# Full-height low-rank products for the decay, and a planner that keeps a waiting unit's step behind the main chain's

## The chip, the cores and the metric

The kernel runs on one core of one Trainium2 chip. The metric is the device time of one execution in microseconds (us); the time of a version is the median of several runs.

## The reference

One block of a hybrid network on a sequence of 1024 tokens with 1024 channels: a normalised and modulated input is projected by `w_in`, a forget-gated attention (8 heads) and an RWKV-7 recurrence (8 heads of 64) work on parts of the projection, their outputs are gated, merged and projected, and a gated convolutional feed-forward part follows. The lines that the change touches:

```python
r, k, v, xw, xa, xg = _split(p, RWKV_SPLITS)           # xw, xa: 64 columns each
w_log = -jax.nn.softplus(-(w0 + jnp.tanh(xw) @ w2)) - 0.5
decay = jnp.exp(-jnp.exp(w_log))
a = jax.nn.sigmoid(a0 + xa @ a2)
g = jax.nn.sigmoid(xg) @ g2
...
def step(state, inp):                                  # over 1024 tokens, 8 heads
    sa = jnp.einsum('bhvk,bhk->bhv', state, a_t)
    state = state * w_t + sa[..., None] * b_t + v_t[..., None] * k_t
    y_t = jnp.einsum('bhvk,bhk->bhv', state, r_t)
```

`w2` and `a2` are 64 x 512, so `tanh(xw) @ w2` and `xa @ a2` are low-rank products with 64 terms in each sum.

## The kernel before

All matrix products of weight are done with operands that are split into a high and a low fp32r half. A product is then hi x hi + hi x lo + lo x hi, three matmuls of 128x512 per 128 terms of the sum.

**Low-rank products.** `w2` is loaded twice into one tile, so that rows 0 to 63 and rows 64 to 127 hold the same 64 weight rows (the first 512 columns belong to the decay, the other 512 to `a`). `w2h` is its high half. `xs2[j]` holds the high half of the activation on 64 rows and its low half on the other 64. One matmul of `w2h` with `xs2[j]` over 128 rows therefore gives hi x hi + hi x lo at once. The third part, lo x hi, uses `w2l` (128x512: the low half of each weight on the 64 rows where `xs2[j]` has its high half) and takes only these 64 rows of both. `lora` runs this for 4 groups of 128 output columns and 2 halves of the sequence; each of the 8 steps issues 4 matmuls (`zp` in the trace) and 2 activations `z` on ScalarE, and then steps aside for 1000 ns of planned time.

**The planner.** The order of TensorE's instructions is written out by the class `Weave`. It keeps a planned clock `now` and a list of chains (Python generators). A chain issues instructions and yields how long its results will take. `run` always takes, among the chains that are due, the one with the lowest priority number; where no chain is due, `fill` issues matmuls of the queue (filler: projections that nothing waits for soon) until the next chain is due. The queue holds the `qk`, `v` and 16 gate projections (48 matmuls each, 24 for either half of the sequence). What of it the recurrence doesn't use is left to the attention; the gates appear as `gt` in the first and as `rk_ps` in the second.

**The recurrence.** Its 8 units (4 head pairs x 2 halves) go through two chains. `pre_chain` (number 2) makes a unit's operands: sums for the norm (`ssq`), masks of the products of `ar` and `bk` (`p`, written to `E`), a solve of 31 steps on VectorE (lines L779 and L781) that goes through DRAM before (`sm`, `M32`) and after (`se`, `TT`), transposes (`vt`, `at`, `tb`), `q`, and a sum `bs`. `main_chain` (number 1) then takes the unit: a transpose `X` of `TT` on VectorE (L836), `xi`, `zi`, `uw`, `mz`, and 8 steps of the state `S` (`sp`, `yp`; the state is scaled on VectorE at L901), then norms `mu` and `va`. While the main chain has no unit it asks again every 200 ns.

Between recurrence and attention, `weave.finish()` issues the rest of the gate that has been begun. The attention of the last head ends the stage, and the merge (`br`) begins.

VectorE, ScalarE, GpSimd and the DMA queue of SyncE are ordered by the tile scheduler in the first two stages, which follows the order in which TensorE's instructions were issued; in the attention VectorE and ScalarE keep the written order.

Of the kernel before, what the change touches and what calls it, by code (L numbers as in the profile page):

```python
# [10 lines left out]
F32R = mybir.dt.float32r  # L11
AF = mybir.ActivationFunctionType
ALU = mybir.AluOpType
# [3 lines left out]
S = 1024  # L17
# [30 lines left out]
class Weave:  # L48
# [27 lines left out]
    def add(self, load, run):  # L76
        self.queue.append((load, run))
# [35 lines left out]

        self.live.append([self.now + wait, 0, chain])

    def run(self, chains):

        self.live = [[self.now, 1 + i, g] for i, g in enumerate(chains)]
        while self.live:
            due = min((c for c in self.live if c[0] <= self.now), key=lambda c: (c[1], c[0]), default=None)  # L120
            if due is None:
                self.fill(min(c[0] for c in self.live))
                continue
            wait = next(due[2], None)
            if wait is None:
                self.live.remove(due)
            else:
                due[0] = self.now + max(wait, 0.0)
# [3 lines left out]
def hybrid_block(ctx: ExitStack, tc: tile.TileContext, a, out):  # L132
    nc = tc.nc
    weave = Weave()
# [11 lines left out]
    def f32(ap):  # L146
        return ap.bitcast(F32)
# [197 lines left out]
    with ExitStack() as es:  # L345
# [54 lines left out]
        HS = (slice(0, 64), slice(64, 128))  # L400
# [4 lines left out]
        xp = lg_st.enter_context(tc.tile_pool(name="xp", bufs=1))  # L405
        xwa = xp.tile([128, S], F32, name="xwa")
        xg = xp.tile([128, S], F32, name="xg")
        w2h = xp.tile([128, S], F32R, tag="w2h", name="w2h")
        w2l = xp.tile([128, 512], F32R, name="w2l")
        g2 = xp.tile([128, 512], F32, name="g2")  # L410


        with tc.tile_pool(name="st", bufs=1) as st, tc.tile_pool(name="stp", bufs=2, space=PS) as stp, \
# [111 lines left out]
            w2 = rp.tile([128, S], F32, tag="raw", name="w2")  # L525
# [19 lines left out]
                for kt in range(KT):  # L545
                    low_part(kt, half, (2,))
            nc.scalar.copy(w2h, w2)
            for j in range(2):
                rs, js = slice(j * 64, j * 64 + 64), slice(j * 512, j * 512 + 512)
                nc.gpsimd.tensor_tensor(w2l[rs, :], w2[rs, js], f32(w2h[rs, js]), op=ALU.subtract)  # L550
            for j, dst in enumerate((xwa, xg)):
                low_out(j, dst)
            nc.scalar.preload_act_table_set("sigmoid_and_others")
# [6 lines left out]
        with tc.tile_pool(name="lg", bufs=1, reuse_waits="tile") as lg, \  # L560
                tc.tile_pool(name="md", bufs=1, reuse_waits="tile") as md:

            xs2 = [lg.tile([128, S], F32R, tag=f"xs{j}", name=f"xs{j}", bufs=1) for j in range(2)]
            for j in range(2):
                rs, ro = slice(j * 64, j * 64 + 64), slice(64 - j * 64, 128 - j * 64)
# [20 lines left out]
            def lora(p, parts):  # L586

                zs = [lg.tile([128, S], F32, tag="z", name=f"z{i}_{p}", bufs=4) for i, _, _, _ in parts]
                for hf in range(2):
                    cs = slice(hf * NH, hf * NH + NH)  # L590
                    pss = [gen(f"zp{i}_{p}{hf}") for i, _, _, _ in parts]
                    for ps, (_, prods, _, _) in zip(pss, parts):
                        for n, (w, x) in enumerate(prods):
                            mm(ps, w[:, p * 128 : p * 128 + 128], x[:, cs], start=n == 0, stop=n == len(prods) - 1)
                    for z, ps, (_, _, _, bias) in zip(zs, pss, parts):
                        if bias is None:
                            nc.vector.tensor_copy(z[:, cs], ps)
                        else:
                            last[:] = [nc.scalar.activation(z[:, cs], ps, AF.Sigmoid, bias=V(bias, p))]
                    if len(parts) > 1 or p > 0:  # L600
                        next(mods, None)
                    yield 1000
                for z, (i, _, _, _) in zip(zs, parts):
                    nc.sync.dma_start(d_lora[i, p], z)
# [3 lines left out]
            def lora_chain():  # L608
                yield 13000
                for p in range(4):  # L610
                    yield from lora(p, [(j, [(w2h[:, j * 512 : j * 512 + 512], xs2[j]), (w2l[HS[j]], xs2[j][HS[j]])], None, b) for j, b in enumerate(("w0", "a0"))])
                use_ln_exp(last[0])
                prods = split_g()
                yield from forget()
                mod_out(2)
                next(mods, None), next(mods, None)
                for p in range(4):
                    yield from lora(p, [(2, prods, None, None)])
                mod_out(5)
                while got[0, 0] < 3:  # L620
                    weave.step()
                yield 0
# [341 lines left out]
        def pre_chain():  # L964
            for k, (p, hf) in enumerate(order):
                while got[p, hf] < 3:
                    weave.step()
                yield from pre(k, p, hf)
                if p < 3:
                    weave.first.extend(rkv_items(p + 1, hf))  # L970
                yield 0

        def main_chain():
            for k, (p, hf) in enumerate(order):
                while (p, hf) not in units:
                    yield 200
                yield from main(k, p, hf)
                yield 0

        weave.run([main_chain(), pre_chain()])  # L980
    rk_st.close()


# [473 lines left out]
    due = []  # L1457
# [514 lines left out]
```

## Time and profile before

| | |
|---|---|
| time, median of 3 runs | 1701.49 us (1699.32 to 1701.51) |
| profiled execution, its own time | 1699.35 us |
| span of the profiled execution | 1697.6 us |
| TensorE busy in the span | 1649.3 us (97%) |
| VectorE / ScalarE / GpSimd busy | 72% / 48% / 8% |
| mean granted clock of TensorE | 0.991 |

The page says that TensorE is busy nearly all the time, and the chain of work that ended last is 82% TensorE. A matmul's record overlaps the next one's, so durations of single matmuls are longer than the time that each adds; the distance from one start to the next is what counts. The stages, by the timeline: up to 75 us load and norm, 75 to 149 the low-rank products among projections, 149 to 645 the recurrence, 645 to 861 the attention, and then the merge and the feed-forward part.

### The profile page before, as it was taken

The page shows a single profiled execution, that of the slowest core. Times are in us where ns is not written, and L with a number is a line of the kernel's source. Part 1 is how long each engine was busy: PE and PEld are TensorE (multiplying, and loading weights), DVE is VectorE, ACT ScalarE, POOL GpSimd, SP SyncE. Part 2 cuts the span into 40 slices and gives each one's busy share as a digit, 9 for nine tenths or more (in the row PEclk, how much of TensorE's full clock was granted, in tenths as well). Part 3 has the DMA queues.
Part 4 walks back from the last instruction along what each step waited for, and adds up shares of the span by engine and source line. Part 5 has one row for each costly group of instructions (what it writes and reads, how often), then busy time and mean ns, then how long its engine had stood idle before and what let it go on. Part 6 is the DMA issues. An engine that isn't in the chain of part 4 may idle for free.

```text
span 1697.6 us, 26285 instructions
## 1 busy us (share of the span) xinstructions
PE 1649.3 (97%) x9886; PEld 1351.7 (80%) x9886; DVE 1218.1 (72%) x2402; ACT 810.7 (48%) x1482; POOL 127.8 (8%) x151
## 2 busy tenths in 40 slices
PE   7999999999999998999989999999999999999998
PEld 7767877787877777888878888888888888888886
DVE  4776787778776624888767534897777777787677
ACT  5553334334354555766732223654444444454455
POOL 0010101111111001212022000000000000000000
PEclk9999999999999999999999999999999999999999
DMA  8487743533332226543177611133332233484463
GB/s 329 145 310 207 194 129 93 137 104 113 99 114 79 93 70 163 145 125 109 39 291 267 223 62 63 50 106 103 121 106 100 93 118 106 158 290 149 128 215 109
DMA packets 120975, 239.87 MB, mean 141 GB/s; under 512 B 39888, under 2 KB 48336, under 8 KB 120848
## 3 DMA queue, kind: packets, MB, share of 16 engines
q1 hardware_dynamic: 112896, 220.94, 39.5%
q0 software_dynamic: 7952, 17.25, 3.8%
q8 instruction: 78, 1.28, 0.3%
q14 instruction: 49, 0.40, 0.1%
HBM read 172.59 MB, written 65.54 MB: 140 GB/s over the span
## 4 chain that ended last, share of the span: by engine, by line
PE 82%; DVE 9%; DMA 4%; ACT 3%; issue 1%; SPq 1%; DVEq 0%; ACTq 0%
PE X L140 13%; PE D L140 12%; PE Y L140 6%; PE gt L140 6%; PE wo L140 5%; PE br L140 5%; PE ps_rkv L140 5%; PE qk L140 4%; PE W L140 3%; PE rk_ps L140 3%; PE v L140 2%; PE ov L140 2%; PE lg L140 2%; PE sp L140 2%; PE tr L140 2%; PE tp L144 2%
## 5 line engine op out<-in xcount | busy, mean ns | idle before, releaser
L140 PE MATMUL D<-op,op 128*128 128x512 f32 x924 | 209.8, 389 | 0.0
L140 PEld LDWEIGHTS D<-op,op 128*128 128x128 f32 x924 | 173.4, 188 | 36.3 <-DVE op L1235 0.3
L140 PE MATMUL X<-T_m,S 128*128 128x512 f32 x440 | 107.2, 390 | 0.2
L140 PEld LDWEIGHTS X<-T_m,S 128*128 128x128 f32 x440 | 82.5, 188 | 18.2 <-ACT x L1511 0.6
L1234 ACT CAST op<-g 128x512 fp32r<-128x512 f32 x77 | 47.8, 621 | 73.4 <-PE D L140 48.3
L1235 DVE TENSOR_TENSOR op<-g,op 128x512 fp32r<-128x512 f32 x77 | 53.0, 688 | 41.3 <-ACT op L1234 41.2
L1471 DVE SCALAR_TENSOR_TENSOR c<-ab,vec,c 128x512 f32<-128x512 f32 x88 | 65.9, 750 | 19.5 <-ACT c L1474 17.9
L779 DVE TENSOR_TENSOR t<-E,M 128x60 f32<-128x60 f32 (+24 forms) x248 | 57.2, 231 | 31.5 <-DMA M<-sm 26.2
L273 DVE TENSOR_TENSOR lo_in<-raw_in,hi_in 128x512 fp32r<-128x512 f32 x84 | 56.4, 706 | 30.0 <-PE gt L140 12.1
L1435 DVE TENSOR_TENSOR S<-ur,S 128x512 fp32r<-128x512 f32 x66 | 45.5, 691 | 35.4 <-ACT S L1431 35.2
L1431 ACT CAST S<-ur 128x512 fp32r<-128x512 f32 x66 | 41.0, 622 | 55.6 <-DVE ur L1424 30.6
L1435 DVE TENSOR_TENSOR A<-ur,A 128x512 fp32r<-128x512 f32 x64 | 44.0, 688 | 31.2 <-ACT A L1431 31.0
L271 ACT CAST hi_in<-raw_in 128x1024 fp32r<-128x1024 f32 x42 | 43.9, 1048 | 46.9 <-PE ps_rkv L140 16.9
L140 PE MATMUL Y<-T_h,A 128*128 128x512 f32 x264 | 63.4, 389 | 0.0
L140 PE MATMUL Y<-T_h,S 128*128 128x512 f32 x264 | 63.3, 389 | 0.0
L1051 ACT ACTIVATE P<-lg,nm 128x896 f32<-128x896 f32 (+3 forms) x64 | 47.5, 743 | 28.6 <-DVE nm L1047 19.6
L140 PE MATMUL X<-B_b,A 128*128 128x512 f32 x252 | 60.8, 390 | 0.0
L140 PE MATMUL W<-B_f,A 128*128 128x512 f32 x252 | 60.6, 389 | 0.0
L781 DVE TENSOR_TENSOR E<-E,t 128x60 f32<-128x60 f32 (+24 forms) x248 | 53.7, 216 | 5.8
L140 PEld LDWEIGHTS Y<-T_h,A 128*128 128x128 f32 x264 | 49.6, 188 | 10.3
L140 PEld LDWEIGHTS Y<-T_h,S 128*128 128x128 f32 x264 | 49.6, 188 | 10.3
L1431 ACT CAST A<-ur 128x512 fp32r<-128x512 f32 x64 | 39.9, 623 | 34.5 <-PE X L140 31.5
(469 smaller groups left out, 4163.9 us busy)
## 6 DMA issues: line engine op xcount, KB each, us to landing
raw_in<-in_w_in SPq DMA_DIRECT2D x50, 512.0 KB, 4.1
wm<-in_w_mod SPq DMA_DIRECT2D x48, 512.0 KB, 6.7
ur<-in_w_up SPq DMA_DIRECT2D x44, 512.0 KB, 4.1
g<-d_g SPq DMA_DIRECT2D x35, 512.0 KB, 3.7
d_g<-gs SPq DMA_DIRECT2D x44, 256.0 KB, 2.0
d_g<-c SPq DMA_DIRECT2D x33, 256.0 KB, 4.5
d_st<-qh SPq DMA_DIRECT2D x64, 128.0 KB, 2.5
d_gate<-gs SPq DMA_DIRECT2D x32, 256.0 KB, 3.0
```

Of the source, the lines that this page charges most:

```text
L140: nc.tensor.matmul(o, lhsT, rhs, start=start, stop=stop, skip_group_check=more)
L144: nc.tensor.transpose(o, i, eye)
L271: nc.scalar.copy(hi, raw)
L273: nc.vector.tensor_tensor(lo[:, c : c + NH], raw[:, c : c + NH], f32(hi[:, c : c + NH]), op=ALU.subtract)
L779: tt(tv, E32[:, 0:J, s : s + 1].to_broadcast([128, J, W]), M32[:, s : s + 1, s + 1 : 32].to_broadcast([128, J, W]), op=ALU.mult)
L781: tt(E32[:, 0:J, s + 1 : 32], E32[:, 0:J, s + 1 : 32], tv, op=ALU.add)
L1051: nc.scalar.activation(e[:, 0:n], lg[:, 0:n], AF.Exp, bias=nm[:, 0:1], accum_out=nm[:, 1:2])
L1234: nc.scalar.copy(hi, src)
L1235: tt(lo, src, f32(hi), op=ALU.subtract)
L1431: nc.scalar.copy(hi, src)
L1435: tt(lo, src, f32(hi), op=ALU.subtract)
L1471: stt(c, ab[:, x + hf * NH : x + hf * NH + NH], V("conv_w", 22 * x + i), c, op0=ALU.mult, op1=ALU.add)
```

## The change

Two edits. The first makes `w2l` a full 128x1024 tile (the low half of both copies of all weights) in another pool, written by one instruction on GpSimd, and takes all 128 rows of it and of `xs2[j]`: hi x lo's missing partner, lo x lo, is added to the sum by it. The second gives `run` an argument `near`: a chain of number 2 that is due is held, with filler instead, as long as a chain of number 1 comes due later than now and sooner than `near` (1300 ns) after the time at which the held chain came due. Only the recurrence passes it.

```diff
-    def run(self, chains):
+    def run(self, chains, near=0.0):
...
+            if near and due[1] == 2:
+                first = min((c[0] for c in self.live if c[1] == 1), default=0.0)
+                if self.now < first < due[0] + near:
+                    self.fill(first)
+                    continue
             wait = next(due[2], None)
...
-        w2l = xp.tile([128, 512], F32R, name="w2l")
...
-            for j in range(2):
-                rs, js = slice(j * 64, j * 64 + 64), slice(j * 512, j * 512 + 512)
-                nc.gpsimd.tensor_tensor(w2l[rs, :], w2[rs, js], f32(w2h[rs, js]), op=ALU.subtract)
...
+            w2l = lg.tile([128, S], F32R, tag="w2l", name="w2l", bufs=1)
+            nc.gpsimd.tensor_tensor(w2l, w2, f32(w2h), op=ALU.subtract)
...
-  [(w2h[:, j * 512 : j * 512 + 512], xs2[j]), (w2l[HS[j]], xs2[j][HS[j]])]
+  [(w2h[:, j * 512 : j * 512 + 512], xs2[j]), (w2l[:, j * 512 : j * 512 + 512], xs2[j])]
...
-        weave.run([main_chain(), pre_chain()])
+        weave.run([main_chain(), pre_chain()], 1300)
```

(The two lines with `w2h` are the lists of products in `lora_chain`, without the rest of the line.)

The order of instructions moves in the recurrence and behind it. Three places follow. The first is on TensorE where the main chain takes the seventh unit (`xi`, `zi` and `uw` with index 0) while the pre chain is at the end of the eighth (`tb`, `q` and `bs` with index 1). Before:

```order
L144 MATMUL tb_11_6040<-cst,bk_1_5674 128x64
L140 MATMUL q_1_6059<-UV_1_5842,E_1_5840 64x64 x16
L140 MATMUL va_1_6010<-Zts_1_6011,blk_r 128x512
L140 MATMUL va_1_6010<-Mts_1_6012,blk_r 128x512
L140 MATMUL xi_0_6097<-X_0_6094,E_0_5165 32x32 x16
L140 MATMUL gt_0_6037<-u_hi,hi_in_5774 128x512 x7
L140 MATMUL gt_0_6037<-u_lo,hi_in_5774 128x512 x5
L140 MATMUL zi_0_6128<-TT_0_5309,X_0_6094 32x32 x16
L140 MATMUL bs_1_6077<-cum_1_6078,blk_r 128x512
L140 MATMUL bs_1_6077<-en_1_6079,blk_r 128x512
```

The same place now, from `va` on (16 rows of `tb` stand where the three dots are):

```order
L146 MATMUL va_1_5948<-Zts_1_5949,blk_r 128x512
L146 MATMUL va_1_5948<-Mts_1_5950,blk_r 128x512
L146 MATMUL xi_0_6093<-X_0_6090,E_0_5311 32x32 x16
...
L146 MATMUL q_1_6132<-UV_1_5882,E_1_5880 64x64 x16
L146 MATMUL zi_0_6155<-TT_0_5463,X_0_6090 32x32 x16
L146 MATMUL gt_1_6068<-u_lo,hi_in_5716 128x512 x7
L146 MATMUL gt_1_6068<-u_hi,lo_in_5717 128x512 x3
L146 MATMUL uw_00_6185<-QA_0_5312,TT_0_5463 64x128 x8
L146 MATMUL uw_04_6197<-QA_0_5312,TT_0_5463 64x128 x8
L146 MATMUL bs_1_6150<-cum_1_6151,blk_r 128x512
L146 MATMUL bs_1_6150<-en_1_6152,blk_r 128x512
```

The next unit's steps have gone behind the main chain's: `tb` and `q` from ahead of `va` and `xi` to behind them, `bs` from behind `zi` to behind `uw`. Counted over the whole recurrence, TensorE goes from a projection or sum (fp32r) to a step of the chains (fp32) or back 223 times instead of 237.

The second place is on TensorE at the end of the attention, the last head (`tp` are transposes of the probabilities, `ov` their products with the values, `rk_ps` the last gate). Before:

```order
L140 MATMUL rk_ps<-u_lo,hi_in_8734 128x512 x7
L140 MATMUL ov<-th_20_9220,vh_8676 128x256
L140 MATMUL ov<-tl_20_9228,vh_8676 128x256
L140 MATMUL ov<-th_20_9220,vh_8676 128x256
L140 MATMUL ov<-tl_20_9228,vh_8676 128x256
L144 MATMUL tp_22_9240<-cst,P_4_9117 128x128
L144 MATMUL tp_22_9240<-cst,P_5_9141 128x128 x2
L140 MATMUL ov<-th_21_9225,vh_8676 128x256
L140 MATMUL ov<-tl_21_9233,vh_8676 128x256
L140 MATMUL ov<-th_21_9225,vh_8676 128x256
L140 MATMUL ov<-tl_21_9233,vh_8676 128x256
L140 MATMUL rk_ps<-u_hi,lo_in_8735 128x512 x7
```

The same place now:

```order
L150 MATMUL tp_22_9247<-cst,P_4_9161 128x128
L150 MATMUL tp_22_9247<-cst,P_5_9184 128x128 x2
L146 MATMUL ov<-th_20_9231,vh_8746 128x256
L146 MATMUL ov<-tl_20_9237,vh_8746 128x256
L146 MATMUL ov<-th_20_9231,vh_8746 128x256
L146 MATMUL ov<-tl_20_9237,vh_8746 128x256
L146 MATMUL ov<-th_21_9245,vh_8746 128x256
L146 MATMUL ov<-tl_21_9252,vh_8746 128x256
L146 MATMUL ov<-th_21_9245,vh_8746 128x256
L146 MATMUL ov<-tl_21_9252,vh_8746 128x256
```

The last gate's matmuls are gone from here. In all, 48 gate matmuls have moved from the attention (336 before, 288 now) into the recurrence and the stretch right behind it (432 before, 480 now). The attention's order on TensorE is the same as before up to the place where the last gate began, and without filler from there on.

The third place is on the DMA queue of SyncE after the input's loads (`raw_in` are columns of `w_in`, `wm` of `w_mod`). Before:

```order
L259 DMA raw_in_643<-in_w_in 128x1024
L259 DMA raw_in_650<-in_w_in 128x1024
L259 DMA raw_in_688<-in_w_in 128x1024
L217 DMA wm_0_759<-in_w_mod 128x1024
L217 DMA wm_1_775<-in_w_mod 128x1024
L217 DMA wm_2_795<-in_w_mod 128x1024
L259 DMA raw_in_726<-in_w_in 128x1024
```

Now:

```order
L265 DMA raw_in_642<-in_w_in 128x1024
L265 DMA raw_in_649<-in_w_in 128x1024
L223 DMA wm_0_758<-in_w_mod 128x1024
L223 DMA wm_1_774<-in_w_mod 128x1024
L223 DMA wm_2_794<-in_w_mod 128x1024
L265 DMA raw_in_687<-in_w_in 128x1024
L632 DMA wr<-in_w_f 128x64
L637 DMA bf<-in_b_f 8x1
L265 DMA raw_in_725<-in_w_in 128x1024
```

The third load of `w_in` has gone behind three loads of `w_mod`, and the fourth, which takes the buffer that `w2` leaves, behind two small ones.

More of the change, by code (lines that the diff above doesn't have):

```diff
@@ L610, in lora_chain @@
                 for p in range(4):
-                    yield from lora(p, [(j, [(w2h[:, j * 512 : j * 512 + 512], xs2[j]), (w2l[HS[j]], xs2[j][HS[j]])], None, b) for j, b in enumerate(("w0", "a0"))])
+                    yield from lora(p, [(j, [(w2h[:, j * 512 : j * 512 + 512], xs2[j]), (w2l[:, j * 512 : j * 512 + 512], xs2[j])], None, b) for j, b in enumerate(("w0", "a0"))])
                 use_ln_exp(last[0])
```

## The prediction

> **What bounds the kernel now.** I read the page first, then the chain of waits, then the timeline of TensorE in the three stretches that the change touches.
>
> ```profile
> span 1697.6 us, 26285 instructions
> PE 1649.3 (97%) x9886; PEld 1351.7 (80%) x9886; DVE 1218.1 (72%) x2402; ACT 810.7 (48%) x1482; POOL 127.8 (8%) x151
> PE 82%; DVE 9%; DMA 4%; ACT 3%; issue 1%; SPq 1%; DVEq 0%; ACTq 0%
> ```
>
> TensorE (PE) is busy 97% of the span and is 82% of the chain that ended last. All matmuls before are there after, so the time can change in three ways only: a matmul takes another time, TensorE waits more or less, or its clock differs. The 48 us of the span in which it isn't busy are the stock that reordering can draw on. In the recurrence (149 to 645 us) the waits of TensorE are, with line, releaser, total, times and longest:
>
> ```profile
> PE xi L140 <- DVE X L836: 3.2, 2, 1.9
> PE sp L140 <- DVE S L901: 3.2, 3, 2.2
> PE at L144 <- DVE E L759: 1.8, 1, 1.8
> PE ps_rkv L140 <- DVE k L368: 1.7, 1, 1.7
> ```
>
> That is 9.9 us in a stage of 496. Whatever the planner's new rule is worth by removing waits, it is not more than that.
>
> **The low-rank products, worked out.** The `zp` tiles, minimum, median and maximum in ns, and how the products stand in the timeline (start, length, instruction):
>
> ```profile
> L140 PE MATMUL zp<-xgs,g2s x24: 389/389/792, 132.4 to 146.0; 128*128 128x512 f32 x24
> L140 PEld LDWEIGHTS zp<-xs,w2h x16: 186/187/188, 89.6 to 110.7; 128*128 128x128 f32 x16
> L140 PE MATMUL zp<-xs,w2h x16: 387/446/502, 89.8 to 110.7; 128*128 128x512 f32 x16
> L140 PEld LDWEIGHTS zp<-xs,w2l x16: 182/182/183, 90.1 to 111.1; 64*128 64x128 f32 x16
> L140 PE MATMUL zp<-xs,w2l x16: 491/498/502, 90.1 to 111.1; 64*128 64x512 f32 x16
> ...
> 80.52 1.98 PE L140 MATMUL ps_rkv<-u_hi,hi_in 128*128 128x512 f32 x8
> 82.33 1.98 PE L140 MATMUL ps_rkv<-u_lo,hi_in 128*128 128x512 f32 x8
> ...
> 92.69 0.39 PE L140 MATMUL zp<-xs,w2h 128*128 128x512 f32 x1
> 93.01 0.49 PE L140 MATMUL zp<-xs,w2l 64*128 64x512 f32 x1
> 93.43 0.50 PE L140 MATMUL zp<-xs,w2h 128*128 128x512 f32 x1
> 93.86 0.50 PE L140 MATMUL zp<-xs,w2l 64*128 64x512 f32 x1
> 94.29 1.43 PE L140 MATMUL ps_rkv<-u_hi,lo_in 128*128 128x512 f32 x5
> 95.56 0.39 PE L140 MATMUL zp<-xs,w2h 128*128 128x512 f32 x1
> ```
>
> A run of 128-row matmuls starts one every (82.33 - 80.52) / 8 = 0.2265 us. In the low-rank step the starts are 0.32, 0.42, 0.43 and 0.43 us apart, and the projections behind it take 1.27 instead of 5 x 0.2265 = 1.13: the step with its 5 projections lasts 95.56 - 92.69 = 2.87 us where 9 evenly spaced matmuls would last 2.04. So changing between 64 and 128 rows costs 0.83 us a step. There are 8 steps (16 `w2h` matmuls, 2 a step), and TensorE waits for nothing else in them: 8 x 0.83 = **6.6 us** less. Bounds: 0, if the distance doesn't come from the 64 rows, and 6.6. I take the full value, because the `zp<-xgs` products, same code, same neighbours and 128 rows, have a median of 389 ns, not 446 or 498.
>
> By the Trainium skill ("TensorE: Matmul & The Clock Gate", sections "LDWEIGHTS (loading the stationary operand)" and "Why this matters for your kernels") a weight load depends on its columns and not on its rows, and a matmul with few rows in the sum takes the same time as one with 128; this term would then be 0. The trace agrees for the load (182 against 187 ns) and not for the matmul (0.43 against 0.2265 us from start to start).
>
> The new `w2l` instruction comes later, since its tile takes memory of the first stage, which is in use until the last low products before 75.08:
>
> ```profile
> L550 POOL TENSOR_TENSOR w2l<-w,w2h x2: 1290/1292/1294, 70.7 to 72.1; 64x512 fp32r<-64x512 f32 x2
> 75.08 1.98 PE L140 MATMUL ps_rkv<-u_hi,hi_in 128*128 128x512 f32 x8
> 73.38 0.33 SPq L259 DMA_DIRECT2D raw_in<-in_w_in  x1
> 86.72 2.12 PE L140 MATMUL ps_rkv<-u_hi,hi_in 128*128 128x512 f32 x8 [0.60 <-DVE k L368]
> ```
>
> Two pieces of 512 columns took 1.29 us each; one of 1024 columns takes 2.6 by columns, 5.2 if twice the elements cost twice. It ends by 80.3 at the latest, and its first reader is at 90.1 (table above), so its cover is 9.8 us and it costs 0. Queued behind it are the one-column copies on GpSimd and, on SyncE, the fourth load of `w_in`, which needs `w2`'s buffer. The third load, now behind three loads of `w_mod`, started at 73.38 and is read at 86.72: 13 us of cover. Both 0; without cover, each us of lateness would be one of TensorE.
>
> **The planner's rule: mode changes.** A change from a projection to a step of the chains is not free even without a wait:
>
> ```profile
> 577.43 1.66 PE L140 MATMUL gt<-u_hi,lo_in 128*128 128x512 f32 x6
> 579.02 0.34 PE L140 MATMUL sp<-UV,E 128*64 128x64 f32 x4
> ```
>
> Six `gt` need 6 x 0.2265 = 1.36 us, and the next start comes after 1.59: 0.23 us for the way there and next to nothing for the way back. The order has 223 such changes instead of 237, so 7 ways there fewer: 7 x 0.23 = **1.6 us** less.
>
> **The 48 gate matmuls that move.** Holding steps makes the recurrence use more filler. 48 matmuls, 48 x 0.2265 = **10.9 us**, come into the recurrence and the stretch behind it: TensorE is nearly always busy there, so they cost their whole time. What the attention's end gives back for them is the open term. Its order is unchanged up to 832.17, so I read what follows:
>
> ```profile
> core 0: us, PE busy (x) PEld busy (x) DVE busy (x) ACT busy (x) POOL busy (x), PEclk, DMA share, GB/s
> 645.40:832.17 186.77, 176.01 (x1077) 153.32 (x1075) 148.41 (x301) 123.44 (x281) 33.54 (x39) 0.99 0.45 124
> 832.17:856.23 24.06, 23.05 (x137) 19.42 (x136) 17.25 (x33) 14.79 (x32) 0.00 (x0) 1.00 0.12 44
> 860.64:863.90 3.26, 3.26 (x8) 2.61 (x9) 0.00 (x0) 0.46 (x1) 2.51 (x2) 0.56 0.87 236
> ...
> 855.83 0.40 PE L140 MATMUL rk_ps<-u_hi,lo_in 128*128 128x512 f32 x1
> 860.64 3.43 PE L140 MATMUL br<-fx,hi_br 128*128 128x512 f32 x8 [4.41 <-ACT hi_br L1208]
> ...
> 856.03 0.37 ACT L1118 COPY o<-ov 64x256 f32<-64x256 f32 x1 [2.06 <-PE ov L140]
> 858.59 0.60 ACT L1131 CAST fx<-o 128x512 fp32r<-128x512 f32 x1
> 859.98 1.12 ACT L1208 CAST hi_br<-raw_br 128x512 fp32r<-128x512 f32 x2
> ...
> 856.43 0.42 DVE L1120 TENSOR_TENSOR o<-o,ov 64x256 f32<-64x256 f32 x1 [1.87 <-ACT o L1118]
> ```
>
> (In rows of stages: length, busy time of each engine with its instructions, granted clock, DMA share, GB/s.) From 832.17 to the first `br` at 860.64 are 28.47 us, and 48 x 0.2265 = 10.9 of them are the gate that moves. Without it TensorE has some 12 us of work here and waits for VectorE and ScalarE instead. Floor: VectorE's own 17.25 us. A stage doesn't reach that: in the attention as a whole VectorE is busy 148.41 of 186.77 us, 79%, and 17.25 / 0.79 = 21.8. I take the middle of 17.25 and 21.8, **19.5 us** to the end of the last `ov`.
>
> Then comes the wait for `hi_br`. The last `ov` ends at 855.83; ScalarE's `o` starts 0.20 later, VectorE's `o` at 856.43 and ends at 856.85; `fx` would need 0.60 and `hi_br` 0.62 of ScalarE. Before, the last gate's activations stood ahead of both and `br` started at 860.64; without them it starts 0.20 + 0.40 + 0.42 + 0.60 + 0.62 + some 0.05 = **2.3 us** after the last `ov`. So the stretch lasts 19.5 + 2.3 = 21.8 instead of 28.47: **6.7 us** back. Ends: 17.25 + 2.3 = 19.6, 8.9 back; or no end of the stretch moves, 0 back.
>
> After the wait of 4.41 us the granted clock was 0.56, and eight `br` matmuls took 3.26 us instead of 8 x 0.2265 = 1.81. If the wait is 2.3 us, I take this restart to go: **1.45 us** less (0 if the clock falls all the same).
>
> **Other moved work.** Filler's weight loads move with it; they run ahead of their use, and at the end SyncE's queue has the last gate's store no longer ahead of the merge's loads: 0. Waits inside the recurrence are dealt anew, since VectorE's order changes with TensorE's; the 9.9 us of the first table say how much is at stake. I take no change, with 4 us either way.
>
> **The sum.** -6.6 (low-rank steps) - 1.6 (mode changes) + 10.9 (48 gate matmuls earlier) - 6.7 (the attention's end) - 1.45 (clock) = **-5.45 us**. Against the profiled execution's 1699.35 us (span 1697.6 and 1.75 around it) that is 1693.9. Its time is at the lower edge of the three runs shown (1699.32 to 1701.51, median 1701.49), and a median is asked, so I put the sum on the median: **1696.0 us**. What a measurement of this kernel can tell from no change is about 0.2%, 3.4 us.
>
> **Rivals.**
>
> *A unit's solve comes too late (slower).* The rule holds a step of the next unit by up to 1.3 us. Up to the load of `M32` that starts the solve a unit has five such steps, so its `X` can come up to 5 x 1.3 = 6.5 us later against the main chain. What there is to spare, at the third unit:
>
> ```profile
> 321.50 0.44 DVE L836 STREAM_TRANSPOSE X<-TT 32x256 f32<-32x256 f32 x1 [0.59 <-DMA TT<-se]
> 328.74 0.69 PE L140 MATMUL xi<-X,E 32*32 32x32 f32 x32
> ```
>
> `X` ends at 321.94 and `xi` starts at 328.74: 6.8 us. For: the margin is nearly the size of the delay, and TensorE, in order, waits with all that is behind `xi`. Against: it takes every step held in full. Price: what the first unit pays in the table of waits, 3.2 us a unit. Four late units: 12.8 - 5.45 = +7.35, 1708.8 us. It decides from 8.9 us on, three units. Chance 0.12.
>
> *The attention's end gives nothing back (same).* If VectorE and ScalarE behind the last head set the end as it is, the 28.47 us and the restart stay: -6.6 - 1.6 + 10.9 = +2.7, 1704.2 us. For: the end is a chain through three engines. Against: VectorE's 17.25 us leave room, and four ScalarE activations of the gate vanish from ahead of `hi_br`. Chance 0.13.
>
> *64 rows cost nothing (same).* If the distance of 0.43 us comes from something else in that stretch, such as its full DMA queues, the first term goes: -5.45 + 6.6 = +1.15, 1702.6 us. The page named above would have it so. Against: neighbours of 128 rows keep 0.2265 there. Chance 0.06.
>
> *The rule removes the waits (faster).* With the main chain's work first on VectorE, all of the 9.9 us but the first unit's 3.2 go: -5.45 - 6.7 = -12.15, 1689.3 us. For: `S` and the masks `E` wait behind a next unit's work on VectorE. Against: nothing keeps other work, such as the weights' low halves, out of VectorE's way. Chance 0.13.
>
> **How the numbers follow.** My sum has 0.52: 0.47 of it faster by over 0.2%, 0.05 within it. The waits removed, 0.13, are faster. Nothing given back, 0.13: 0.10 within, 0.03 slower. 64 rows free, 0.06: within. Late solve, 0.12: slower. What is left, 0.04, is a handful of small new waits that add up: slower. Faster 0.60, within 0.2% 0.21, slower 0.19. The range goes from the waits removed, 1688, to nothing given back, 1705; it leaves out the late solve, the small waits and the edges of the others, some 2 in 10.
>
> **What would show it.** Low-rank steps: 64x512 is gone from `zp`, starts are 0.2265 us apart, and what follows stands 6 to 7 us earlier at about 112 us. The recurrence's end then comes some 3 us later than before (-6.6 - 1.6 + 10.9, part of it behind the end). The stretch from `lg` of the last head to `br` shows waits of TensorE of some 7 us where there was one of 4.41, and the first `br` runs at full clock. I am wrong if `zp` keeps its distances, if TensorE's waits in the recurrence leave 9.9 us by more than 4, or if that last stretch lasts under 19 or over 25 us.

## The result, and the profile after

The changed kernel takes 1710.46 us (median of 6 runs, 1708.94 to 1714.42) against 1701.1 us before: ratio 1.0061, 95% interval 1.0048 to 1.0075. It is slower by some 9 us; 1696.0 and a range up to 1705 had been forecast. (The 1701.1 us are the median of six runs of the kernel before, three more than in the table ahead.)

The part on the low-rank products did what was said. Of `zp`'s 16 products with `w2l`, the starts before ran from 90.1 to 111.1 us; after (the tile's group on TensorE: min/median/max ns, first and last start):

```profile
L146 PE MATMUL zp<-xs,w2l x16: 389/389/389, 88.0 to 102.8; 128*128 128x512 f32 x16
```

No 64-row matmul is left, and the 21.0 us are 14.8. The loss is behind that. TensorE's stages before (stretch, its length, busy time and instructions of each engine, granted clock, DMA share, GB/s): the filler ahead of the first unit's `vt`, the recurrence to the last `sp`, from there to the first `rk_ps`, from that to the first `lg`, the attention to its last `lg`, from that to the first `br`:

```profile
146.40:178.80 32.40, 32.40 (x161) 25.62 (x160) 18.87 (x28) 10.97 (x18) 2.92 (x4) 1.00 0.77 221
178.80:632.90 454.10, 443.48 (x4151) 353.53 (x4151) 319.67 (x937) 197.38 (x347) 50.19 (x69) 1.00 0.38 110
632.90:647.90 15.00, 15.00 (x73) 12.37 (x74) 4.20 (x6) 9.69 (x15) 6.45 (x7) 1.00 0.46 138
647.90:661.20 13.30, 10.09 (x45) 8.02 (x44) 4.03 (x6) 5.37 (x9) 2.15 (x4) 1.00 1.17 262
661.20:841.10 179.90, 172.26 (x1070) 150.56 (x1069) 151.50 (x310) 122.13 (x282) 29.80 (x35) 0.99 0.37 106
841.10:860.60 19.50, 14.21 (x91) 12.10 (x89) 10.91 (x20) 13.39 (x28) 0.00 (x0) 0.99 0.12 41
```

The same six stages after, then the first eight `br` and the first 2.5 us behind the longest wait:

```profile
138.80:178.40 39.60, 39.60 (x192) 31.61 (x192) 19.98 (x30) 13.16 (x21) 5.03 (x9) 1.00 0.78 228
178.40:640.40 462.00, 443.85 (x4141) 355.63 (x4141) 325.69 (x939) 199.37 (x350) 49.77 (x69) 0.99 0.38 105
640.40:661.60 21.20, 21.20 (x100) 17.52 (x99) 6.17 (x9) 12.05 (x20) 8.11 (x9) 1.00 0.70 189
661.60:679.70 18.10, 11.88 (x44) 9.35 (x44) 2.58 (x4) 5.35 (x9) 0.38 (x1) 0.81 0.76 195
679.70:858.30 178.60, 168.90 (x1051) 147.47 (x1050) 150.16 (x307) 122.20 (x282) 28.80 (x34) 0.99 0.34 98
858.30:871.50 13.20, 9.90 (x62) 8.28 (x61) 9.87 (x19) 8.07 (x18) 0.00 (x0) 0.87 0.26 76
871.50:874.80 3.30, 3.30 (x9) 2.57 (x10) 0.14 (x1) 0.46 (x1) 2.51 (x2) 0.57 0.99 338
673.48:676.00 2.52, 2.52 (x6) 2.04 (x7) 1.37 (x3) 1.72 (x3) 0.00 (x0) 0.50 0.23 66
```

The ledger of the two spans (1697.6 and 1707.2 us): -7.7 up to the first `f` of the forget gate (105.1 instead of 112.8), +7.3 from there to the first `vt`, +7.9 in the recurrence, +6.2 to the first `rk_ps`, +4.8 to the first `lg`, -7.6 in the rest of the attention, -1.3 from `br` to the end: +9.6. Filler accounts for part of it. The order puts 32 more matmuls ahead of the recurrence; by the rows 27 more stand behind it (100 instead of 73), which leaves 11 fewer in it; together these are the 48 that left the attention. The recurrence thus lasts 7.9 us longer with 2.5 us (11 x 0.2265) less to do. TensorE stood for 18.15 us in it instead of 10.62 (length less busy time), and it was busy 443.85 us instead of 443.48 although it had those 2.5 us less to do. What it takes for the same matmuls is called pace below. TensorE's waits, by name (us, times, longest), of the whole execution:

```profile
PE rk_ps L146 <- ACT gm L1161: 7.4, 3, 6.2
PE sp L146 <- DVE S L905: 5.5, 5, 2.0
PE ps_rkv L146 <- DVE t L783: 5.1, 1, 5.1
PE uw L146 <- ACT TT L856: 4.0, 2, 2.8
PE br L146 <- ACT hi_br L1212: 2.1, 1, 2.1
```

Two places stand out: `ps_rkv` and `uw` in the recurrence, which waited for other things or not at all before, and `rk_ps` at the beginning of the attention.

**In the recurrence, VectorE stands before a load.** Around the second `uw` wait, in the timeline (start, duration, what ended the wait in brackets):

```profile
444.23 1.72 SPq L775 DMA_DIRECT2D M<-sm  x4
...
449.59 0.19 DVE L783 TENSOR_TENSOR t<-E,M 128x31 f32<-128x31 f32 x1 [7.14 <-DMA M<-sm]
450.04 0.69 DVE L345 SCALAR_TENSOR_TENSOR gs<-gt,gs 128x512 f32<-128x512 f32 x1
450.76 0.63 ACT L346 ACTIVATE gs<-gs 128x512 f32<-128x512 f32 x1 [3.35 <-DVE gs L345]
451.30 0.73 ACT L856 COPY TT<-zi 32x256 f32<-32x256 f32 x2
451.70 0.43 PE L146 MATMUL uw<-QA,TT 64*64 64x128 f32 x2 [2.78 <-ACT TT L856]
```

The first instruction of a next unit's solve stands next on VectorE and waits 7.14 us for `M`. Behind it stands the gate's `gs`; for that ScalarE waits, and behind ScalarE's `gs` stands the copy of `TT` that the main chain's `uw` needs. The wait of `ps_rkv` has the same source by a longer way, in the timeline 100 us earlier:

```profile
330.40 0.19 DVE L783 TENSOR_TENSOR t<-E,M 128x31 f32<-128x31 f32 x1 [5.66 <-DMA M<-sm]
333.33 0.69 DVE L938 TENSOR_TENSOR o<-y,gg 128x512 f32<-128x512 f32 x1
334.05 0.34 SPq L939 DMA_DIRECT2D d_orw<-o  x1
334.97 0.51 SPq L712 DMA_DIRECT2D cum<-d_lora  x1
339.49 1.23 DVE L715 TENSOR_TENSOR_SCAN cum<-cst,cum 128x512 f32<-128x512 f32 x1 [0.77 <-DMA cum<-d_lora]
340.74 0.63 ACT L718 ACTIVATE el<-cum 128x512 f32<-128x512 f32 x1 [2.51 <-DVE cum L715]
341.80 1.98 ACT L277 CAST hi_in<-raw_in 128x1024 fp32r<-128x1024 f32 x2
342.88 3.06 PEld L146 LDWEIGHTS ps_rkv<-u_hi,hi_in 128*128 128x128 f32 x8 [5.35 <-ACT hi_in L277]
```

VectorE stands 5.66 us before `M`, so `o` comes late; SyncE's queue holds the store of `o` and behind it the load of `cum`; ScalarE waits for `cum`, and behind its `el` and `en` stands the cast `hi_in` of the weights that the projection needs. (The table of waits names a `t` of VectorE that ended at about the same time; the weight load of the same matmul, the last row, names `hi_in`.)

VectorE's whole wait for `M` (us, times, longest), after and then before:

```profile
DVE t L783 <- DMA M<-sm: 31.3, 7, 7.1
```

```profile
DVE t L779 <- DMA M<-sm: 26.2, 7, 5.5
```

The stall is not new, but what stood behind it was needed less.

**The clock makes these waits dearer.** Three slices of the recurrence in the changed kernel:

```profile
300.00:350.00 50.00, 44.64 (x486) 39.80 (x485) 33.87 (x105) 17.22 (x35) 5.16 (x8) 0.97 0.41 111
450.00:500.00 50.00, 48.30 (x348) 38.02 (x349) 39.95 (x117) 21.41 (x33) 6.89 (x11) 0.97 0.33 101
500.00:550.00 50.00, 47.92 (x465) 36.37 (x465) 38.33 (x109) 26.24 (x46) 6.38 (x7) 0.97 0.24 69
```

In the kernel before the same three stretches of time have a granted clock of 1.00. Within them the clock falls behind three waits: in the 3.4 us behind that of 5.14 us (`ps_rkv`) it was 0.50, behind that of 2.78 us (`uw`) 0.56, and behind one of 1.97 us for `S` at 530.02, which was not traced to `M`, it was 0.59. As an estimate from the rows, 3 x 50 x 0.03 = 4.5 us of the pace are lost so.

**At the junction, the gate's stores meet two heads' loads.** The queues of GpSimd and SyncE and ScalarE's waits, in the timeline:

```profile
651.61 0.72 POOL L997 DMA_DIRECT2D stA<-d_st  x1
...
654.23 0.32 SPq L347 DMA_DIRECT2D d_gate<-gs  x1
...
659.75 8.71 SPq L347 DMA_DIRECT2D d_gate<-gs  x2
...
664.81 0.60 ACT L342 ACTIVATE gs<-gt 128x512 f32<-128x512 f32 x1 [5.08 <-DMA d_gate<-gs]
672.34 0.60 ACT L1160 ACTIVATE gs<-rk_ps 128x512 f32<-128x512 f32 x1 [4.22 <-DMA d_gate<-gs]
```

GpSimd issues head 1's load at 651.61, right behind head 0's at 649.32; before, a cast of a weight stood between the two (642.19, cast 646.31, 647.29), and fewer gate products lay there. The gate's stores are under way beside 4.26 MB of loads, ScalarE waits twice for a store to give its buffer back, and TensorE waits 6.22 us for `gm`. After that wait the granted clock was 0.50 for 2.5 us. The kernel before has the same 4.26 MB here and one such wait of ScalarE (4.16 us); TensorE's wait was 3.21 us, and the clock behind it stayed at 1.00.

### The profile page after: what moved, and what is told of

Same layout as the page of the kernel before. It is cut to its first block, busy times and chain, and to the rows that moved or that the text cites. A ratio compares the mean times of both kernels' runs of the same rounds, so it can differ in the third digit from the quotient of the medians.

```text
span 1707.2 us, 26300 instructions
## 1 busy us (share of the span) xinstructions
PE 1648.2 (97%) x9886; PEld 1357.9 (80%) x9886; DVE 1225.3 (72%) x2402; ACT 810.7 (47%) x1481; POOL 124.7 (7%) x149
## 4 chain that ended last, share of the span: by engine, by line
PE 60%; DVE 4%; ACT 2%; DMA 1%; issue 1%; ACTq 0%
PE X L146 13%; PE D L146 12%; PE Y L146 6%; PE wo L146 5%; PE br L146 5%; PE W L146 3%; PE gt L146 3%; PE rk_ps L146 3%; PE lg L146 2%; PE ov L146 2%; PE tp L150 2%; PE tr L146 1%; DMA d_gate<-gs 1%; DVE tl L1091 0%; DVE nm L1051 0%
## 5 line engine op out<-in xcount | busy, mean ns | idle before, releaser
L146 PEld LDWEIGHTS X<-T_m,S 128*128 128x128 f32 x440 | 82.4, 188 | 18.2 <-ACT T_m L1664 0.6
L783 DVE TENSOR_TENSOR t<-E,M 128x60 f32<-128x60 f32 (+24 forms) x248 | 58.7, 237 | 37.2 <-DMA M<-sm 31.3
L1475 DVE SCALAR_TENSOR_TENSOR c<-ab,vec,c 128x512 f32<-128x512 f32 x88 | 65.9, 750 | 19.5 <-ACT c L1478 17.9
L1055 ACT ACTIVATE P<-lg,nm 128x896 f32<-128x896 f32 (+3 forms) x64 | 47.4, 743 | 31.4 <-DVE nm L1051 21.7
L146 PE MATMUL ps_rkv<-u_hi,hi_in 128*128 128x512 f32 x192 | 52.1, 405 | 5.1 <-DVE t L783 5.1
```

The costliest lines, as they stand in the source:

```text
L146: nc.tensor.matmul(o, lhsT, rhs, start=start, stop=stop, skip_group_check=more)
L783: tt(tv, E32[:, 0:J, s : s + 1].to_broadcast([128, J, W]), M32[:, s : s + 1, s + 1 : 32].to_broadcast([128, J, W]), op=ALU.mult)
L1055: nc.scalar.activation(e[:, 0:n], lg[:, 0:n], AF.Exp, bias=nm[:, 0:1], accum_out=nm[:, 1:2])
L1475: stt(c, ab[:, x + hf * NH : x + hf * NH + NH], V("conv_w", 22 * x + i), c, op0=ALU.mult, op1=ALU.add)
```

## The experiments

Time is the median; ratio is to runs of the kernel before on the same chip. "Stood" is length less TensorE's busy time in the recurrence, "junction" the stretch from the first `rk_ps` to the first `lg`. The recurrence holds 11 filler matmuls, 2.5 us, less than before in the kernels with the whole rule, some 20 less in the two `nopoll` kernels, and some 12 more in `poll_only`. The three columns on the right are each from one profiled execution, which can lie some us off the median (that of `rows_m7000` took 1697.6 us, against a median of 1693.4). `grouped64` ran once, so it has no interval.

| kernel | us | ratio (95%) | recurrence, us | stood, us | junction, us |
|---|---|---|---|---|---|
| before | 1698.7 to 1701.2 | 1 | 454.1 | 10.6 | 13.3 |
| changed | 1710.5 | 1.0061 (1.0048 to 1.0075) | 462.0 | 18.2 | 18.1 |
| rows_only | 1693.2 | 0.9960 (0.9948 to 0.9972) | 454.8 | 11.1 | 16.3 |
| near_only | 1715.1 | 1.0087 (1.0072 to 1.0103) | 461.1 | 16.7 | 21.7 |
| nopoll | 1698.2 | 0.9985 (0.9975 to 0.9995) | 454.0 | 14.1 | 17.3 |
| poll_only | 1698.2 | 0.9988 (0.9977 to 0.9999) | 459.0 | 11.2 | 17.4 |
| head_late | 1702.9 | 1.0005 (0.9992 to 1.0018) | 462.5 | 19.0 | 11.3 |
| after_m5000 | 1692.4 | 0.9964 (0.9950 to 0.9978) | 444.4 | 6.5 | 18.9 |
| rows_head3 | 1689.3 | 0.9947 (0.9932 to 0.9962) | 455.3 | 10.4 | 11.2 |
| rows_m7000 | 1693.4 | 0.9967 (0.9955 to 0.9979) | 458.4 | 11.8 | 16.1 |
| after_m5000_head | 1686.7 | 0.9934 (0.9917 to 0.9952) | 446.6 | 6.8 | 11.3 |
| rows_m7000_head3 | 1690.9 | 0.9944 (0.9930 to 0.9957) | 456.6 | 10.9 | 11.3 |
| nopoll_both | 1684.8 | 0.9912 (0.9896 to 0.9928) | 442.7 | 6.3 | 14.4 |
| grouped64 | 1697.0 | one run | 456.3 | 11.6 | 15.0 |

**The two edits apart.** `rows_only` is the changed kernel without the argument:

```diff
-        weave.run([main_chain(), pre_chain()], 1300)
+        weave.run([main_chain(), pre_chain()])
```

> The kernel before with only the low-rank part: full w2l, all 128 rows, no holding. The order of TensorE is that of before to the last instruction. Theory A (the low-rank part does what the prediction said, and the loss is all the rule's): zp starts 0.2265 us apart, first f some 7 us earlier, every later stage as long as before; 1701.1 - 6.6 = 1694.5 us. Rival B (what is saved there is waited for later, since VectorE's and ScalarE's chains in the recurrence do not get faster): waits in the recurrence grow from 10.5 by the same 6.6, 1701.

Theory A holds: 8.0 us faster by the medians (4.8 to 8.8 by the interval). One stage is longer than before, the junction (16.3 instead of 13.3 us with the same order): its wait of 3.65 us is little longer than the 3.21 of before, but the clock behind it was 0.50. `near_only` has the argument and the old `w2l`.

> The kernel before with only the rule (near = 1300) and the 64-row low-rank products of before. Order of TensorE as in the changed kernel. Theory A (the two parts add): 1710.5 + 6.6 = 1717 us, with waits in the recurrence of some 18 us instead of 10.5, the stretch from the first rk_ps to the first lg 18 instead of 13.3 us. Rival B (the rule hurts only because the earlier low-rank end moved the program against its loads): 1701 to 1706.

Theory A again: 13.9 us slower by the medians, with 16.7 us of standing in the recurrence; the junction took 21.7 us, more than the 18 said. The rule alone costs more than the low-rank edit brings.

**Two kinds of holds.** While the main chain has no unit it asks every 200 ns, and to the rule each asking is a step that is due soon. By the planner's own clock that holds eight steps of the first unit for some 1.1 us each; the other 26 holds, for 0.05 to 1.3 us, are behind real steps of the main chain. `nopoll` keeps only the real ones, `poll_only` (with `and self.poll` in the same place) only the others:

```diff
                 while (p, hf) not in units:
+                    weave.poll = True
                     yield 200
+                weave.poll = False
...
-            if near and due[1] == 2:
+            if near and due[1] == 2 and not self.poll:
```

> The changed kernel, but a step is not held while the main chain only asks whether its next unit is there (its 200-ns polling). In the order the gate's products stand as before again (432 in the recurrence and behind, 336 in the attention). Theory A (the polling holds move the filler, and with it the gate's stores into the head's loads): the stretch first rk_ps to first lg is 13 us again, waits in the recurrence are back to 8 to 12 us: 1694 to 1697 us. Rival B (holding behind the main chain's real steps makes loads and masks late): waits in the recurrence stay at 16 to 20 us and only the 4.8 us of the junction come back: 1704 to 1706.

> The counterpart of the kernel without the polling holds: full w2l, and the rule holds a step only while the main chain polls for a unit (eight steps of the first unit, 8.8 us together by the planner's clock), never behind a real step of the main chain. In the order 32 more filler matmuls stand ahead of the recurrence and 48 gate matmuls leave the attention, as in the changed kernel. Theory A (the two kinds of holds add): 1693.2 + (1710.5 - 1698.2) = 1705.5 us, with the junction at 18 us and some 15 us of waits in the recurrence. Rival B (the polls only move filler, which costs nothing by itself; the loss needs both kinds): 1693 to 1697.

In the order of `nopoll` no gate product moves (432 `gt` and 336 `rk_ps`, as before); in that of `poll_only` all 48 do, with 32 more `qk` ahead of the recurrence. So the polls alone move the filler. On time neither A held: each kind by itself costs some 0.25% over `rows_only` (0.9960), where both together cost 1.0%. The sum would be 0.9960 + 0.0025 + 0.0028 = 1.0013, and the changed kernel has 1.0061. With polls alone TensorE stands no longer than in `rows_only` (11.2 against 11.1 us), with real holds alone 3 us longer. The two interact: the wait of 5.1 us of `ps_rkv` is 1.8 us with polls alone and split into three waits of 1.2 us in all with real holds alone, that of `uw` (4.0) is 0.5 and 2.1.

**The junction.** `head_late` changes only where GpSimd issues the three loads of head 1 (`ds` and `i`):

```diff
-            i = nc.gpsimd.tensor_copy(hi, raw)
+            i = marks["cast"] = nc.gpsimd.tensor_copy(hi, raw)
...
+        for d in (*ds, i) if h == 1 else ():
+            tc.add_manual_dep(d.ins, marks["cast"].ins.name, NOSYNC)
```

> The changed kernel, in which GpSimd issues the loads of head 1 behind its first cast of a late gate weight, as it stood in the kernel before; the order of TensorE, VectorE and ScalarE stays. Theory A (the gate's stores crawl beside two heads' loads, and ScalarE waits for their buffers): the wait of rk_ps for gm falls from 6.2 us to under 1.5, the clock behind it stays 1.0; 1710.5 - 5 = 1705.5 us. Rival B (the stores are slow beside head 0's load alone, or the collision only moves to head 1's later load): the wait stays or reappears at the next gate; 1708 to 1711.

The stretch, in the rows of stages, and then ScalarE in the timeline:

```profile
664.90:676.20 11.30, 10.10 (x45) 8.03 (x44) 2.59 (x4) 5.36 (x9) 2.11 (x4) 1.00 0.96 229
```

```profile
666.42 0.60 ACT L342 ACTIVATE gs<-gt 128x512 f32<-128x512 f32 x1 [3.42 <-DMA d_gate<-gs]
...
670.59 0.60 ACT L1162 ACTIVATE gs<-rk_ps 128x512 f32<-128x512 f32 x1 [0.85 <-PE rk_ps L146]
```

Theory A, and a little more: ScalarE's second wait is for TensorE and no longer for a store, `rk_ps` waits 1.20 us, the clock stays at 1.00, and the stretch takes 11.3 us instead of 18.1. The same is to be had without the rule, one cast later (`load_head(1)` at `k % 4 == 3`):

> The low-rank part alone, with head 1's loads issued behind the second late cast of GpSimd, some 17 us later than before. Order of TensorE as before. Theory A (two heads' loads together slow the gate's stores, for which ScalarE waits; TensorE waits 3.65 us and then runs 3.6 us at a granted clock near 0.5): the stretch first rk_ps to first lg falls from 16.3 to some 11 us: 1693.2 - 5.2 = 1688 us. Rival B (head 1 comes too late, or the next gate's store meets its load): a wait of lg or rk_ps for 3 to 6 us at 665 to 680 us; 1692 to 1696.

Theory A: 11.2 us, no new wait at head 1. So the collision is there without the rule as well (5.1 us of the stretch, 6.8 with it). In the whole time the gain without the rule is not clear of the intervals (0.9947 against 0.9960, which overlap).

**VectorE's stall.** `after_m5000` leaves TensorE's order as it is. It issues the solve 5 us of planned time later, with its GpSimd instructions and its stores and loads behind it, and ties its first instruction on VectorE to stand behind what the chains have given VectorE until then; the load of `M` itself stays:

```diff
+            def solve():
...
+                    before = marks["dve"]
-                tt(tv, E32[:, 0:J, s : s + 1].to_broadcast([128, J, W]),
+                    i = tt(tv, E32[:, 0:J, s : s + 1].to_broadcast([128, J, W]),
...
+                    if s == 0:
+                        tc.add_manual_dep(i.ins, before.ins.name, NOSYNC)
...
+            weave.spawn(solve(), 5000)
```

> The changed kernel with the order of TensorE untouched; on VectorE the first instruction of a unit's solve stands behind whatever the chains have given VectorE in the next 5 us of the planner's clock, so that VectorE no longer waits for the load of M with the main chain's y, QA, o and Wt behind it. Theory A (the recurrence loses its time because VectorE stands 4 to 7 us before M in every unit, and the later alignment puts TensorE's next steps behind that): VectorE's wait for M falls from 31.3 us to under 12, the waits of ps_rkv (5.1) and uw (4.0) go, those for S shrink: 8 us less, 1702.5. Rival B (the solve is what is late: X, then xi, come later by what VectorE does first): xi waits grow by 1 to 3 us a unit; 1710 to 1720. Rival C (TensorE's waits come from ScalarE's and SyncE's queues, not from VectorE): 1708 to 1711.

VectorE's wait for `M` (`t` has a helper's line here), and the recurrence:

```profile
DVE t L157 <- DMA M<-sm: 3.7, 2, 3.1
```

```profile
178.60:623.00 444.40, 437.87 (x4140) 351.54 (x4139) 326.91 (x939) 198.98 (x350) 49.87 (x69) 1.00 0.38 109
```

Theory A, at twice its size: the wait falls from 31.3 to 3.7 us, and with the same order of TensorE the recurrence takes 17.6 us less, 11.6 of them waits and 6.0 pace (`uw`'s waits are gone, that of `ps_rkv` is 1.9 us, those for `S` 0.4; the granted clock is 1.00 where it was 0.99, and 1.00 in each of the three slices that had 0.97). `X` does not come late: `xi` waits 2.2 us in all, against 2.3. The same edit without the rule (7 us, since without the holds 5 move it in one unit only):

> The low-rank part alone (no holding), with the solve's first VectorE instruction behind what the chains give VectorE in the next 7 us of the planner's clock (5 us would move it in one unit only, since without the holds the main chain's VectorE work comes later). TensorE's order is that of before. Theory A (VectorE's 26 to 31 us of standing before M cost TensorE time in both kernels): M's wait falls from 27.6 us to under 8, the recurrence from 454.8 us by 6 to 9; ratio to before 0.991 to 0.993, some 1686 us. Theory B (only the changed kernel's alignment exposes these waits): the recurrence stays at 452 to 456 us, ratio 0.995 to 0.997.

The same two views:

```profile
DVE t L157 <- DMA M<-sm: 6.3, 1, 6.3
```

```profile
172.90:631.30 458.40, 446.57 (x4153) 356.87 (x4153) 321.95 (x937) 197.19 (x347) 48.94 (x69) 0.99 0.38 109
```

Theory B: VectorE's wait is cut from 27.6 to 6.3 us, and the recurrence gains nothing (458.4 against 454.8; the ratio is 0.9967 against 0.9960). In the order of before, taking the stall away brings nothing; in that of the changed kernel it brings more than the recurrence had lost.

**Both places mended.**

> The changed kernel with both places mended: the solve behind 5 us of the chains' work on VectorE, head 1's loads behind the first late cast. TensorE's order as in the changed kernel. If the two places add: 1692.4 - 7.6 = 1685 us, the recurrence 444 us, the stretch first rk_ps to first lg 11 to 13 us. If they do not (the earlier end of the recurrence only waits at the loads): 1690 to 1692.

> The same two places mended without the rule: full w2l, no holding, solve behind 7 us of work, head 1's loads behind the second late cast. Theory A (M's wait costs in both kernels, the rule in itself is worth nothing): 1689.3 - 7 = 1682 us, as fast as or faster than the changed kernel with both mended. Theory B (only the holds' alignment exposes the wait): 1687 to 1691, and the changed kernel with both mended wins, so that the rule itself is worth 3 to 6 us once VectorE is free.

> The rule without the polling holds, and both places mended (solve behind 5 us of the chains' work on VectorE, head 1's loads behind the second late cast). Order of TensorE as in the kernel without the polling holds. Theory A (the rule's real holds are worth something once VectorE is free; the polls only push 7 us of filler ahead of the first unit): waits in the recurrence fall from 14.1 to 6 to 8 us, the junction to 11 us; ratio to before 0.989 to 0.992, the fastest of all. Theory B (with both places mended the deal of the order no longer matters): ratio 0.993 to 0.995, as the changed kernel with both mended (0.9934) and the low-rank part with late head loads (0.9947).

The places add (1686.7 us against a forecast of 1685). The two kernels of the first two texts are not apart by their intervals, so they don't show that the rule is worth something; `nopoll_both` (real holds alone, both places mended) has the lowest ratio of all, 0.9% (0.7 to 1.0) under before. Its interval lies just under those of the kernels without the rule, `rows_m7000_head3` and `rows_head3`, and overlaps that of `after_m5000_head`: that taking out the polls brings anything once both places are mended is not shown. Its recurrence, and the first 3 us behind its wait at the junction:

```profile
174.20:616.90 442.70, 436.36 (x4132) 350.28 (x4132) 323.15 (x936) 194.40 (x343) 50.96 (x69) 1.00 0.39 112
645.00:648.00 3.00, 3.00 (x9) 2.32 (x8) 1.90 (x3) 1.31 (x3) 0.00 (x0) 0.51 0.03 10
```

With the same order as `nopoll` (454.0 us) its recurrence takes 11.3 us less. So the rule's real holds seem to be of use where VectorE is free for the main chain, some 0.3% as theory A said (against kernels whose solve was moved by 7 us or not at all, not by 5); its junction stayed at 14.4 instead of 11 us, a wait of 2.8 us and a slow clock behind it.

**What the 64 rows cost.** `grouped64` is the kernel before with a step's products in the order `w2h`, `w2h`, `w2l`, `w2l`:

```diff
-                    for ps, (_, prods, _, _) in zip(pss, parts):
-                        for n, (w, x) in enumerate(prods):
+                    for n in range(len(parts[0][1])):
+                        for ps, (_, prods, _, _) in zip(pss, parts):
+                            w, x = prods[n]
```

> The kernel before with the four products of a low-rank step in another order: both 128-row products, then both 64-row ones (each accumulates as before). Theory A (what costs is the change between 64 and 128 rows): two changes a step instead of four, some 2.4 us a step with its five neighbours instead of 2.87, the third row free of it at 0.23 us. Rival B (a 64-row matmul costs 0.43 us wherever it stands): 0.43 for each 64-row product, 2.45 too, but with starts 0.23, 0.23, 0.43, 0.43. Rival C (every product of this stretch is slow, by its operands): 2.87 as before.

```profile
92.08 0.62 PE L140 MATMUL zp<-xs,w2h 128*128 128x512 f32 x2
92.63 0.50 PE L140 MATMUL zp<-xs,w2l 64*128 64x512 f32 x2
93.06 1.43 PE L140 MATMUL ps_rkv<-u_hi,lo_in 128*128 128x512 f32 x5
94.33 0.61 PE L140 MATMUL zp<-xs,w2h 128*128 128x512 f32 x2
```

None of the three: a step with its five neighbours takes 2.25 us (92.08 to 94.33) instead of 2.87. The two 64-row products lie in one stretch of 0.50 us, though one alone lasts 0.498: they use rows 0 to 63 and 64 to 127 and ran side by side. The way from 128 to 64 rows costs some 0.1 us (0.55 from the first start to the third for two products), the pair 0.43 together, and the way back some 0.14 (1.27 for five projections instead of 1.13). From the first `zp` to the last are 16.3 us (89.8 to 106.1), where the kernel before has 21.3 and the changed one 15.0: order alone gives 5.0 of 6.3 us of this stretch. What it gives of the whole time, one run (1697.0 us, against a median of 1698.7 before on the same chip) can't tell.

## Why the prediction was wrong

- **Low-rank steps, -6.6 us: right.** The `zp` stretch shrank by 6.2 us, and `rows_only` gained 8.0 (4.8 to 8.8). The cause is narrower than "changing between 64 and 128 rows": `grouped64` has two such changes a step and pays 0.21 us, so most of the 0.83 came from lone 64-row products between full ones.
- **48 gate matmuls, +10.9 us: right in size, wrong in cause.** 32 + 27 - 11 = 48 matmuls stand earlier. It was put down to the holding of steps in general; it is the polls before the first unit alone (`nopoll` moves none).
- **The attention's end, -6.7 us: right, with some luck,** since its 19.5 us were the middle between a floor and a guess. From the first `lg` to the first `br` 199.4 us became 191.8, 7.6 less; the wait for `hi_br` was 2.08 us where 2.3 had been worked out.
- **The clock at `br`, -1.45 us: wrong, 0.** The first eight `br` took 3.30 us at a clock of 0.57, as before, though the wait was half as long.
- **Mode changes, -1.6 us: neither shown nor refuted.** TensorE's busy time in the recurrence rose by 0.4 us with 2.5 us less work, 2.9 us of pace. The slower clock alone accounts for some 4.5 (the estimate above), which leaves -1.6; that is a remainder of rounded rows and no measurement.
- **"Waits inside the recurrence ... I take no change, with 4 us either way": the step that failed.** They grew by 7.5 us, and the pace cost 2.9 more (7.9 + 2.5 - 7.5), since the clock fell behind three of them; the prediction had counted the clock only at `br`. Its own sign of being wrong, waits more than 4 us off 9.9, came true. The table of TensorE's waits of before gave 9.9 us as what was at stake; the larger stock was in VectorE's table, 26.2 us before `M`, which TensorE's order happened to hide. `after_m5000` shows that the loss goes with this stall: without it, in the same order, the recurrence takes 17.6 us less.
- **Moved work "0" at the junction: the second step that failed, +4.8 us.** The gates' stores were followed to the end of the attention, not to its beginning, where GpSimd's loads lie. `head_late` shows the collision: without it the stretch takes 11.3 us. But the moved gates are not the whole of the 4.8: `rows_only`, which moves none, has 3.0 of them, mostly by the clock behind its wait. That the kernel before got away with 13.3 us in its profile was luck of the clock, which no term of the prediction allowed for.
- **The rivals.** The late solve gave 1708.8 us, near the measured time, but for another reason: `xi` waited 2.3 us, less than the 3.2 of before. What happened was nearest to "small new waits that add up", with 0.04. "The rule removes the waits" comes true only in kernels where VectorE is not kept by `M`.

The terms -6.6 + 10.9 - 6.7 come out at -6.2 + 10.9 - 7.6 = -2.9; waits and pace in the recurrence add 10.4, the junction 4.8, what the start-up and the merge gave by themselves -1.5 and -1.3: +9.5, against +9.6 of the spans (rounding).

Why the two kinds of holds cost more together than one by one was not traced hold by hold; shown is only that the loss of the pair goes with VectorE's stall.

## What to carry to other kernels

An engine that waits for a load in every round is a risk even where this costs nothing now: before instructions are put in another order, read what is queued behind each long wait on the engines that are not the bottleneck, since the new order decides whether the bottleneck needs it. When a planner's rule asks "is something due soon", see whether idle polling counts as due. And moved work is followed with its stores as well, to the place where they meet other transfers.

## What the runs showed of the hardware

- Two 64-row matmuls on opposite halves of the rows ran side by side, 0.43 us for the pair, and alternating them with 128-row ones cost 0.83 us a step more than the full height. The Trainium skill ("TensorEngine Tiling (Array Packing)", section "Key Properties") says that a change of tiling mode drains TensorE and that different tiles can run in parallel; both agree with these rows.
- The granted clock does not follow the length of the wait before it alone. Behind 3.21 us before it was 1.00, behind 3.65 us in the same place of `rows_only` 0.50 (the junction took 3.0 us more for the same order), behind 2.78 us in `nopoll_both` 0.51, and behind 2.08 us at `br` 0.57. Waits for `S` in the recurrence show both outcomes too: 1.00 behind 2.23 us in the kernel before (at 300.68), 0.59 behind 1.97 us in the changed one. The Trainium skill ("TensorE: Matmul & The Clock Gate", section "What's actually happening") speaks of a free-running window of some 3.4 us and has the clock fall after an idle one. Both outcomes at like lengths agree with a window that runs freely; that waits of 1.97 to 2.78 us were enough does not agree with one that has to be idle throughout.

```profile
649.26:651.26 2.00, 2.00 (x5) 1.61 (x6) 0.85 (x2) 1.21 (x3) 0.00 (x0) 0.50 0.94 288
```

The row is `rows_only`, right behind its wait: five matmuls in 2.00 us, 0.4 us each instead of 0.2265.
